# A hybrid decoder layer on one core: block order at the mixer's input, held layer-norm steps and held attention heads

## Chip, core and metric

The kernel runs on one core of a Trainium2 chip, in one launch. The metric is the device time of that core in microseconds (us): the median of three runs of the kernel. A profile of one further execution gives the spans of its instructions.

## The reference

One layer with x of 256 tokens by 2048 channels, float32:

```
x <- LN1(alpha*x + 0.5*SwiGLU_1(x))
x <- LN2(alpha*x + W_out [DiffAttn(x) || RWKV7(x)])
x <- LN3(alpha*x + 0.5*SwiGLU_2(x))
```

SwiGLU has 5632 hidden channels: `(silu(x @ w_gate) * (x @ w_up)) @ w_down`. One projection `w_in` makes the columns of both mixers. The differential attention has 8 heads, each with two softmaxes over causal scores with a linear bias; their difference multiplies v, and each head is normalised. RWKV7 has 16 heads of 64 channels with this state recursion over the tokens:

```
sa = einsum('bhvk,bhk->bhv', state, -kk_t)
state = state * w_t + sa[..., None] * (kk_t * a_t) + v_t[..., None] * k_t
y_t = einsum('bhvk,bhk->bhv', state, r_t)
```

The decay w, the rate a and the gate g come from a small block of low-rank columns of `w_in` (64 + 64 + 160 = 288 columns).

## The kernel before

Every float32 product is made of three matmuls of halves: the operand is cast to a high half (wh for weights, xh for activations) and the rest is kept as a low half (wl, xl); L153, L154 and L155 multiply high by high, high by low and low by high.

The weights are streamed through `Stream.block`: for each pair of 128-row tiles of a column block (512 or 288 columns wide), SP loads them (L133, three buffers `raw`), ScalarE (ACT) casts wh (L143), VectorE (DVE) subtracts wl (L146, called the split below), and TensorE (PE) runs six matmuls for the first 128 tokens (tt = 0) and, `lag` pairs later, six for the other 128 (tt = 1). wh and wl have five slots in the mixer and seven in the feed-forward parts; `buffers(nw, lag)` sets both numbers.

Beside the stream run generators: the heads of the attention (`attn_heads`, two generators of two heads for each group of four heads; g is the group) and the RWKV groups (`rwkv_group`, two groups of eight heads). `run_bg` advances them after each pair of the stream, by credits in the first part of the mixer, and in the output projection's first two parts ("even", set at L1160) by one step per pair; a count in `stream.hold` makes a generator sit out so many pairs there. `yield None` gives the turn back without a step. In the even part, PE's order is the order in which the code was written; all other engines' orders, and PE's elsewhere, are set by the scheduler. Each engine works through its own list in order, and a DMA stands in the list of the engine that issues it.

The mixer streams, in this order: the 288 low-rank columns, then the RWKV columns k (i = 1), r (0) and v (2) of group 0, then attention q/k and the rest. The rwkv groups invert triangular blocks on DVE (L834, L836, for j = 31 down to 1; U and Y are 64 x 1024 tiles), copy the transpose (L839) and send both through DRAM: ACT issues dY (L840) and dYT (L841), and, when these have landed, the gathers TT (L849) and YT (L853). L862 is the matmul that reads YT, L873 the one that reads TT.

The output projection runs in three parts over the sources (0 and 2: first attention group and first RWKV group; 1: the second attention group; 3: the second RWKV group). L1136 adds the residual to the first part's accumulator. In the last part `ln_stats` (L330 add, L332 statistics) and `ln_tail` (L337 to L361) normalise: two rounds of centring (L345) and scaling (L353), and each scaled quarter y is transposed by PE (L83), cast (L89, xh) and its rest subtracted (L90, xl).

Of the kernel before, what the change touches and what calls it, by code (L numbers as in the profile page):

```python
# [13 lines left out]
ALU = mybir.AluOpType  # L14
# [16 lines left out]
LAG = {"ffn": 4, "mix": 2}  # L31
NW = {"ffn": 7, "mix": 5}
# [7 lines left out]
def build(tc, A, out):  # L40
# [15 lines left out]
    def nm(s):  # L56
        uid[0] += 1
        return f"{s}_{uid[0]}"

    V, SC, G, T = nc.vector, nc.scalar, nc.gpsimd, nc.tensor  # L60
# [14 lines left out]
    def fill(n=1):  # L75
        for f in late[:n]:
            f()
        del late[:n]

    def transpose_split(src, tt, q, store, on_dve=False, put_off=False):  # L80
        tr = tr_bank[-1](True)
        for j in range(4):
            T.transpose(tr[:, j, :], src[:, j * P:(j + 1) * P], ident)  # L83
        split(tr, store, tt, q, on_dve, put_off)
# [14 lines left out]
    class Stream:  # L99
# [13 lines left out]

        def phase(self, name, pool, banks=None):
            assert not self.pend
            self.name, self.pool, self.banks, self.slot, self.rot = name, pool, banks, 0, 0
            self.buffers(NW[name], LAG[name])

        def buffers(self, nw, lag):
# [206 lines left out]
    stream = Stream()  # L326
    KX = [(k, k) for k in range(16)]

    def ln_stats(tt, y, acc, st, n):
        V.tensor_tensor(out=y, in0=y, in1=acc, op=ALU.add)  # L330
        fill(tt)
        V.bn_stats(out=st[:, n, :], in_=y)  # L332
        fill(tt)

    def ln_tail(tt, y, st, gt, bt, last):
        mv = sp.tile([P, 2], F32, tag="mv", name=nm("mv"))
        V.bn_aggr(out=mv, in_=st)  # L337
        ve = sp.tile([P, 1], F32, tag="ve", name=nm("ve"))
        V.tensor_scalar(out=ve, in0=mv[:, 1:2], scalar1=LN_EPS, scalar2=None, op0=ALU.add)
        rs = sp.tile([P, 1], F32, tag="rs", name=nm("rs"))  # L340
        G.tensor_tensor(out=rs, in0=ve, in1=neghalf, op=ALU.pow)
        fill(tt)

        def center(q):
            V.scalar_tensor_tensor(out=y[q], in0=y[q], scalar=mv[:, 0:1], in1=gt[q], op0=ALU.subtract, op1=ALU.mult)  # L345
            fill(tt)

        center(0)
        center(1)
        for q in range(4):  # L350
            c = slice(q * NB, (q + 1) * NB)
            yq = y[q]
            i = V.scalar_tensor_tensor(out=yq, in0=yq, scalar=rs, in1=bt[q], op0=ALU.mult, op1=ALU.add)  # L353
            if q < 2:
                with tc.issue_after(i.ins):
                    center(q + 2)
            if last:
                nc.sync.dma_start(out=out[tt * P:(tt + 1) * P, c], in_=yq)
            else:
                transpose_split(yq, tt, q, xT, put_off=tt == 0)  # L360
                nc.scalar.dma_start(out=xs[tt][:, c], in_=yq)  # L361
        if tt == 0 and not last:
            stream.behind = [None] * 2 + [i.ins] * 5
# [195 lines left out]
    def mix(mp, pq, C):  # L559
        vB, om = C["vB"], C["om"]  # L560

        def bank(tag, shape=(P, NB)):
            return pq.tile(list(shape), F32, tag=BANKS[tag][0], name=nm(tag), bufs=BANKS[tag][1])

        w_in = A["w_in"][0]
        R0 = 3 * AW
# [10 lines left out]
        def chan_major(acc, tt, widths, dst):  # L577
            tot = sum(widths)
            tm = mp.tile([P, NB], F32, tag="tm", name=nm("tm"), bufs=2)
            SC.copy(out=tm[:, :tot], in_=acc[:, :tot])  # L580
            tr = bank("tr", (P, 4, P))
            o = 0
            for i, w in enumerate(widths):
                T.transpose(tr[:w, i, :], tm[:, o:o + w], ident)  # L584
                o += w
            dst(tr)

        def shift(praw, i, mi, dst, n=P):
            df = mp.tile([P, S], F32, tag="itmp", name=nm("df"))
            SC.activation(out=df[:n], in_=praw[:n, i, 0:S], func=AF.Copy, scale=vB[:n, mi:mi + 1])  # L590
            x1 = praw[:n, i, 1:S + 1]
            d = df[:n]
            if len(dst.shape) == 3:
                x1 = x1.rearrange("p (c t) -> p c t", c=4)
                d = d.rearrange("p (c t) -> p c t", c=4)
            V.scalar_tensor_tensor(out=dst, in0=x1, scalar=om[:n, mi:mi + 1], in1=d, op0=ALU.mult, op1=ALU.add)
# [27 lines left out]
                SC.activation(out=g2[0:32], in_=g2[0:32], func=AF.Sigmoid)  # L624
                lora.update(tw=tw, g1=g1, g2=g2)

        stream.block(w_in, R0 + 3072, 288, KX, x_lhs, lora_done)

        res = {}

# [16 lines left out]
        def rwkv_start(g, prev=None):  # L647
            gr = Group(g)
            st = {"prev": prev, "group": gr}
            if prev is not None:  # L650
                prev["next"] = st
            st["gen"] = rwkv_group(g, st)
            stream.spawn(st["gen"], BG)
            return st

        def rwkv_cols(g, st, parts):
            gr = st["group"]

            def done(tt, acc, i):
                if tt == 0:  # L660
                    pr = hp.tile([P, 4, S + 1], F32, tag="J1" if g == 0 and i == 2 else "H3", name=nm("praw"))
                    V.memset(pr[:, :, 0:1], 0.0)
                    st["raw"] = pr
                pr = st["raw"]
                chan_major(acc, tt, [P] * 4, lambda tr: SC.copy(out=pr[:, :, 1 + tt * P:1 + (tt + 1) * P], in_=tr))
                if tt == 1:
                    for p in range(4):
                        d = (gr.rh[:, p], gr.ka[:, p], gr.vv[:, p, :])[i]
                        shift(pr, p, 8 * i + 4 * g + p, d)
                    st["rkv"[i]] = True  # L670
                    if i == 2:
                        st["gen2"] = rwkv_values(g, st)
                        stream.spawn(st["gen2"], BG)

            for i in parts:
                stream.block(w_in, R0 + i * AW + g * NB, NB, KX, x_lhs, lambda tt, acc, i=i: done(tt, acc, i))
# [320 lines left out]
        def attn_cols(g):  # L997
            st = {"q": qq[:, g],
                  "k": hp.tile([P, 4, S], F32, tag=HT["k"], name=nm("k"))}

            def qkdone(tt, acc, n):
                chan_major(acc, tt, [P] * 4, lambda tr: SC.copy(out=st[n][:, :, tt * P:(tt + 1) * P], in_=tr))
                if n == "q" and tt == 1:
                    st["left"] = 2
                    st["gens"] = [attn_heads(g, st, (i, i + 2)) for i in range(2)]
                    for x in st["gens"]:
                        stream.spawn(x, AT)

            stream.block(w_in, AW + g * NB, NB, KX, x_lhs, lambda tt, acc: qkdone(tt, acc, "k"))
            stream.block(w_in, g * NB, NB, KX, x_lhs, lambda tt, acc: qkdone(tt, acc, "q"))  # L1010
            return st

        def attn_heads(g, st, heads):
            q, k = st["q"], st["k"]
            W = 3 * P
            spans = [slice(0, P), slice(P, W)]
            for h in heads:
# [23 lines left out]
                for qb in range(2):  # L1041
                    V.tensor_scalar(out=s[:, 0, spans[qb]], in0=s[:, 0, spans[qb]], scalar1=rr[:, qb, 0:1], scalar2=None, op0=ALU.mult)
                    V.scalar_tensor_tensor(out=s[:, 0, spans[qb]], in0=s[:, 1, spans[qb]], scalar=rr[:, qb, 1:2],
                                           in1=s[:, 0, spans[qb]], op0=ALU.mult, op1=ALU.add)
                yield 0.6
                tr = bank("at", (P, 4, P))
                for b in range(3):
                    T.transpose(tr[:, b, :], s[:, 0, b * P:(b + 1) * P], ident)
# [35 lines left out]
                for qb in range(2):  # L1084
                    T.transpose(tr[:, qb, :], ot[:, qb, :], ident)
                V.tensor_scalar(out=q[:, h, :], in0=tr[:, 0:2, :].rearrange("p a b -> p (a b)"), scalar1=C["ng"], scalar2=None, op0=ALU.mult)
                yield 0.6
            st["left"] -= 1
            if st["left"] == 0:
                res[g] = q  # L1090
# [2 lines left out]
            return [g for st in sts for g in [st.get("gen"), st.get("gen2")] + st.get("gens", []) if g is not None]  # L1093

        r1 = rwkv_start(0)
        rwkv_cols(0, r1, (1, 0, 2))
        r2 = rwkv_start(1, r1)
        a1 = attn_cols(0)
        rwkv_cols(1, r2, (1, 0))
# [3 lines left out]
        a2 = attn_cols(1)  # L1103
# [16 lines left out]
        st = [sp.tile([P, 4, 6], F32, tag=f"st{t}", name=nm("st"), bufs=1) for t in range(2)]  # L1120
# [10 lines left out]
        def o_done(tt, acc, n, i):  # L1131
            c = slice(n * NB, (n + 1) * NB)
            if i == 0:
                rc = mp.tile([P, NB], F32, tag="tm", name=nm("rc"), bufs=2)
                nc.scalar.dma_start(out=rc, in_=xs[tt][:, c])
                V.scalar_tensor_tensor(out=y[tt][n], in0=rc, scalar=ALPHA, in1=acc, op0=ALU.mult, op1=ALU.add)  # L1136
            elif i < len(parts) - 1:
                V.tensor_tensor(out=y[tt][n], in0=y[tt][n], in1=acc, op=ALU.add)
            else:
                ln_stats(tt, y[tt][n], acc, st[tt], n)  # L1140
                if n == 3:
                    ln_tail(tt, y[tt], st[tt], gb[0], gb[1], False)

        y = []
# [8 lines left out]
            for n in range(4):  # L1153
                stream.block(A["w_out"][0], n * NB, NB, ks, o_lhs, lambda tt, acc, n=n, i=i: o_done(tt, acc, n, i))

        stream.hold = {g: 2 * i + 2 for i, g in enumerate(a2["gens"])}
        for i, qs in enumerate(parts):
            for q in qs:
                ready(q)
# [85 lines left out]
```

## Time and profile before

| | us |
|---|---|
| runs | 1914.72, 1918.86, 1919.4; median 1918.86 |
| profiled execution | 1916.35, span of its instructions 1914.6 |
| TensorE (PE) idle in the span | 30.6 |
| mean clock granted to TensorE | 0.994 of full speed |

A row of a timeline has the start (us from the span's start), the length, the engine, the line, the operation, the tiles as out<-in, shapes, and in brackets the idle time ahead of it with what ended it. ACTq is ACT issuing a DMA. A row of windows has the stretch, its length, then for PE, PE's weight loads, DVE, ACT and POOL the busy time and the number of instructions, the granted PE clock, the share of the DMA engines and the GB/s. PE's matmuls are pipelined, so their rows overlap.

### The profile page before, as it was taken

How to read it: one execution, taken by the hardware profiler on the slowest of the kernel's cores; microseconds unless marked ns; L12 is line 12 of the kernel's file. 1: busy time of each engine (PE TensorE's matmuls, PEld its weight loads, DVE VectorE, ACT ScalarE, POOL GpSimd, SP SyncE). 2: the span in 40 equal slices, each digit the busy share in tenths (PEclk: the TensorE clock that was granted, in tenths of full speed). 3: DMA queues.
4: the chain of work that ended last, by engine and by line, in shares of the span. 5: the costliest groups of instructions: out<-in, count | busy, mean ns of one | idle time of the engine just before them, and what ended most of it. 6: DMA issues, size and time to landing. Idle time of an engine off the chain costs nothing.

```text
span 1914.6 us, 24935 instructions
## 1 busy us (share of the span) xinstructions
PE 1884.0 (98%) x9335; PEld 1549.9 (81%) x9335; DVE 1624.3 (85%) x1834; ACT 1094.7 (57%) x1376; POOL 72.7 (4%) x110
## 2 busy tenths in 40 slices
PE   9999999999999999999999999999999999999997
PEld 7888888888888888887778778788888888888886
DVE  8999987789999976777678777999999778999995
ACT  6656664556666536656554544566666545666651
POOL 0000101100000000000000000000000110000000
PEclk9999999999999999999999999999999999999999
DMA  9756676665667456555435545775566676566743
GB/s 313 247 200 217 187 239 220 229 215 200 217 212 232 144 171 199 167 161 150 143 117 159 162 145 193 262 247 198 200 210 226 218 235 211 196 210 209 232 151 132
DMA packets 207320, 381.72 MB, mean 199 GB/s; under 512 B 23530, under 2 KB 25648, under 8 KB 206944
## 3 DMA queue, kind: packets, MB, share of 16 engines
q1 hardware_dynamic: 182928, 350.53, 55.4%
q0 software_dynamic: 6832, 15.32, 3.0%
q10 hardware_dynamic: 17440, 14.29, 2.6%
q8 instruction: 73, 1.20, 0.2%
q14 instruction: 47, 0.39, 0.1%
HBM read 368.29 MB, written 11.80 MB: 199 GB/s over the span
## 4 chain that ended last, share of the span: by engine, by line
PE 58%; DVE 3%; DMA 1%; issue 1%; ACT 1%; ACTq 0%; DVEq 0%
PE acc L154 17%; PE acc L153 17%; PE acc L155 17%; DVE wl L146 1%; PE sm L789 1%; DVE y L345 0%; PE tr L443 0%; DVE y L353 0%; PE tr L584 0%; PE at L1027 0%; PE pr L731 0%; DMA U<-dU 0%; PE sm L898 0%; PE sm L890 0%; DMA dY<-Y 0%
## 5 line engine op out<-in xcount | busy, mean ns | idle before, releaser
L143 ACT CAST wh<-raw 128x1024 fp32r<-128x1024 f32 (+2 forms) x833 | 853.6, 1049 | 597.4 <-PE acc L155 379.2
L146 DVE TENSOR_TENSOR wl<-raw,wh 128x1024 fp32r<-128x1024 f32 (+2 forms) x833 | 984.6, 1216 | 206.7 <-ACT wh L143 202.5
L154 PE MATMUL acc<-wl,xh 128*128 128x512 f32 (+1 forms) x1552 | 606.2, 392 | 2.0 <-DVE wl L146 2.0
L155 PE MATMUL acc<-wh,xl 128*128 128x512 f32 (+1 forms) x1552 | 604.3, 391 | 0.4 <-DVE xl L90 0.4
L153 PE MATMUL acc<-wh,xh 128*128 128x512 f32 (+1 forms) x1552 | 600.0, 394 | 2.0 <-ACT xh L89 1.8
L153 PEld LDWEIGHTS acc<-wh,xh 128*128 128x128 f32 x1552 | 292.6, 189 | 63.4 <-ACT xh L89 2.8
L154 PEld LDWEIGHTS acc<-wl,xh 128*128 128x128 f32 x1552 | 292.8, 189 | 61.8 <-DVE wl L146 3.6
L155 PEld LDWEIGHTS acc<-wh,xl 128*128 128x128 f32 x1552 | 292.7, 189 | 60.6 <-issue 0.7
L224 DVE TENSOR_TENSOR raw<-raw,raw 128x2048 f32<-128x2048 f32 x112 | 256.3, 2288 | 2.2 <-DMA raw<-in_ffn_w_gate_dram 1.7
L154 PE MATMUL acc<-wl,hh 128*128 128x512 f32 x544 | 212.0, 390 | 0.0
L155 PE MATMUL acc<-wh,hh 128*128 128x512 f32 x544 | 211.4, 389 | 0.0
L153 PE MATMUL acc<-wh,hh 128*128 128x512 f32 x544 | 210.9, 390 | 0.0
L153 PE MATMUL acc<-wh,s 128*128 128x512 f32 x448 | 174.9, 390 | 1.0 <-ACT acc L250 1.0
L155 PE MATMUL acc<-wh,s 128*128 128x512 f32 x448 | 174.6, 390 | 0.0
L154 PE MATMUL acc<-wl,s 128*128 128x512 f32 x448 | 174.5, 389 | 0.0
L153 PEld LDWEIGHTS acc<-wh,hh 128*128 128x128 f32 x544 | 102.1, 188 | 21.7 <-ACT wh L143 0.4
L154 PEld LDWEIGHTS acc<-wl,hh 128*128 128x128 f32 x544 | 102.2, 188 | 21.1
L155 PEld LDWEIGHTS acc<-wh,hh 128*128 128x128 f32 x544 | 102.2, 188 | 20.9
L153 PEld LDWEIGHTS acc<-wh,s 128*128 128x128 f32 x448 | 84.1, 188 | 19.1 <-ACT acc L250 1.5
L154 PEld LDWEIGHTS acc<-wl,s 128*128 128x128 f32 x448 | 84.1, 188 | 17.6 <-DVE wl L146 0.3
L155 PEld LDWEIGHTS acc<-wh,s 128*128 128x128 f32 x448 | 84.1, 188 | 17.4
L237 ACT COPY acc<-acc 128x512 f32<-128x512 f32 x28 | 16.0, 571 | 50.8 <-PE acc L155 47.0
(264 smaller groups left out, 1098.3 us busy)
## 6 DMA issues: line engine op xcount, KB each, us to landing
raw<-in_ffn_w_up_dram SPq DMA_DIRECT2D x176, 512.0 KB, 5.3
raw<-in_ffn_w_down_dram SPq DMA_DIRECT2D x176, 512.0 KB, 5.3
raw<-in_ffn_w_gate_dram SPq DMA_DIRECT2D x175, 512.0 KB, 4.6
raw<-in_w_in_dram SPq DMA_DIRECT2D x96, 512.0 KB, 3.6
raw<-in_w_out_dram SPq DMA_DIRECT2D x32, 512.0 KB, 4.1
sd<-s POOLq DMA_DIRECT2D x16, 256.0 KB, 4.0
s<-sd POOLq DMA_DIRECT2D x16, 256.0 KB, 5.1
xs<-y ACTq DMA_DIRECT2D x16, 256.0 KB, 2.5
```

The source lines that it names most:

```text
L143: SC.copy(out=wh[:, c, :w], in_=raw[:, c, :w])
L146: self.cut = V.tensor_tensor(out=wl[:, c, :w], in0=raw[:, c, :w], in1=wh[:, c, :w].bitcast(F32), op=ALU.subtract).ins
L153: T.matmul(a, hi, wh[:, j, :w], start=first and j == 0, stop=False, skip_group_check=True)
L154: T.matmul(a, hi, wl[:, j, :w], start=False, stop=False, skip_group_check=True)
L155: i = T.matmul(a, lo, wh[:, j, :w], start=False, stop=last and j == 1, skip_group_check=True)
L224: V.tensor_tensor(out=out, in0=x, in1=y, op=ALU.subtract)
L237: SC.copy(out=u, in_=a)
L789: T.matmul(pe[e][:, c, :], BK[r, p, c, e:e + 2].rearrange("p a t -> p (a t)"), AR[r, p, c].rearrange("p a t -> p (a t)"), start=True, stop ...
```

## The change

Six edits. (1) At the start of a phase the slot number of wh and wl goes on from where it was, modulo five, instead of 0. (2) In LN2, the second token half's last add and its last two statistics operations are held until the first half's second scaling has been issued (`stream.scaled`). (3) At the mixer's input the key block of 512 columns comes first, with a lag of four pairs; the block of 288 columns is second, then r and v. (4) The heads of the second attention group stop ahead of their transposes until the even part has begun. (5) At the end of a head of that group (of its first two heads) stand three yields for one. (6) The counts in `stream.hold` are one lower.

```diff
         def phase(self, name, pool, banks=None):
-            self.name, self.pool, self.banks, self.slot, self.rot = name, pool, banks, 0, 0
+            self.name, self.pool, self.banks, self.slot, self.rot = name, pool, banks, self.slot % NW["mix"], 0
...
-    def ln_stats(tt, y, acc, st, n):
-        V.tensor_tensor(out=y, in0=y, in1=acc, op=ALU.add)
-        fill(tt)
-        V.bn_stats(out=st[:, n, :], in_=y)
-        fill(tt)
+    def ln_stats(tt, y, acc, st, n, behind=None):
+        def held(on):
+            return tc.issue_after(behind) if on and behind is not None else ExitStack()
+
+        with held(n == 3):
+            V.tensor_tensor(out=y, in0=y, in1=acc, op=ALU.add)
+            fill(tt)
+        with held(n >= 2):
+            V.bn_stats(out=st[:, n, :], in_=y)
+            fill(tt)
...
+            if q == 1 and tt == 0:
+                stream.scaled = i.ins
...
-        stream.block(w_in, R0 + 3072, 288, KX, x_lhs, lora_done)
...
                 yield 0.6
+                while g == 1 and not stream.even:
+                    yield None
                 tr = bank("at", (P, 4, P))
                 for b in range(3):
                     T.transpose(tr[:, b, :], s[:, 0, b * P:(b + 1) * P], ident)
...
-                yield 0.6
+                for i in range(3 if g == 1 and h < 2 else 1):
+                    yield 0.6
...
         r1 = rwkv_start(0)
-        rwkv_cols(0, r1, (1, 0, 2))
+        stream.buffers(NW["mix"], NW["mix"] - 1)
+        rwkv_cols(0, r1, (1,))
+        stream.buffers(NW["mix"], LAG["mix"])
+        stream.block(w_in, R0 + 3072, 288, KX, x_lhs, lora_done)
+        rwkv_cols(0, r1, (0, 2))
...
-                ln_stats(tt, y[tt][n], acc, st[tt], n)
+                ln_stats(tt, y[tt][n], acc, st[tt], n, stream.scaled if tt == 1 and n >= 2 else None)
...
-        stream.hold = {g: 2 * i + 2 for i, g in enumerate(a2["gens"])}
+        stream.hold = {g: 2 * i + 1 for i, g in enumerate(a2["gens"])}
```

Lines of the changed kernel that are spoken of: L840, L842 and L845 are the inversion and the copy (L834, L836, L839 before), L846, L847, L855 and L859 the DMAs dY, dYT, TT and YT, L868 the matmul on YT (L862 before), L879 the one on TT, L1149 the residual's add (L1136 before), L334 and L337 the norm's add and statistics, L350 and L358 centring and scaling, L1048, L1049 and L1056 a head's scaling, its difference of softmaxes and its transposes.

The places where the lists of the built programs differ most follow. A row has the line, the operation, tiles as out<-in with the numbers of the buffers, and the size.

**The end of the second group's inversion, on DVE.** Before (y_9223 stands later in the list):

```order
L836 TENSOR_TENSOR Y_8112<-Y_8112,itmp_8454 64x2x30
L146 TENSOR_TENSOR wl_9228<-raw_9225,wh_9227 128x1024
L1033 TENSOR_SCALAR mx_9019<-mx_9019 128x4
L834 TENSOR_TENSOR itmp_8505<-U_8110,Y_8112 64x31
L836 TENSOR_TENSOR Y_8112<-Y_8112,itmp_8505 64x31
L839 COPY U_8110<-Y_8112 64x1024
L146 TENSOR_TENSOR wl_9251<-raw_9248,wh_9250 128x1024
L1029 SCALAR_TENSOR_TENSOR s_9030<-dist,at_9034 128x384
```

The same place in the changed kernel:

```order
L1149 SCALAR_TENSOR_TENSOR y_9211<-rc_9347,acc_9219 128x512
L842 TENSOR_TENSOR Y_8112<-Y_8112,itmp_8454 64x2x30
L1080 TENSOR_SCALAR vr_9327<-ss_9326 128x2
L840 TENSOR_TENSOR itmp_8505<-U_8110,Y_8112 64x31
L1083 TENSOR_SCALAR fl_9328<-vr_9327 128x2
L1085 SCALAR_TENSOR_TENSOR fl_9328<-vr_9327,fl_9328 128x2
L842 TENSOR_TENSOR Y_8112<-Y_8112,itmp_8505 64x31
L845 COPY U_8110<-Y_8112 64x1024
L1086 TENSOR_TENSOR ars_9329<-ars_9329,fl_9328 128x4
L1087 TENSOR_TENSOR ars_9329<-ars_9329 128x2
L146 TENSOR_TENSOR wl_9526<-raw_9523,wh_9525 128x1024
```

The last two steps and the copy stood ahead of the output projection's first results; now they stand behind the add that takes the first of them (acc_9219), and the second group's first softmaxes (s_9018 and s_9030, before behind the copy in part) are ahead of them.

**The DMAs behind it, on ACT.** Before:

```order
L840 DMA dY_8104<-Y_8112 64x1024
L841 DMA dYT_8105<-U_8110 32x1024
L991 COPY v_8972<-acc_8979 128x512
L849 DMA TT_9238<-dY_8104 32x16x32
L89 CAST xh_9217<-og_8637 128x512
L849 DMA TT_9238<-dY_8104 32x16x32 x3
L853 DMA YT_9244<-dYT_8105 32x16x32 x2
L1037 ACTIVATE s_9030,ssum_9032<-s_9030,mx_9031 128x128 x2
```

In the changed kernel:

```order
L1148 DMA rc_9569<-xs_83 128x512
L143 CAST wh_9525<-raw_9523 128x1024
L846 DMA dY_8104<-Y_8112 64x1024
L847 DMA dYT_8105<-U_8110 32x1024
L855 DMA TT_9226<-dY_8104 32x16x32 x4
L859 DMA YT_9232<-dYT_8105 32x16x32 x2
L874 COPY Q<-AR_6648 64x16x64 x2
L1058 COPY pT_9405<-at_9401 128x384
```

The softmax of s_9030 stood behind YT and now stands ahead of dY; between the four DMAs nothing else is left. On PE, the matmul that reads YT (L862 before, L868 now) stands in both programs behind the same 12 weight matmuls: six for acc_9231 (now acc_9219), whose last one ends that accumulation, and six for the next accumulator.

**LN2, on DVE.** The names y_9223 and y_9224 (before), y_9211 and y_9212 (now) are the halves' quarters of the output. Before:

```order
L332 BN_STATS st_9204<-y_9224 128x6
L332 BN_STATS st_9203<-y_9224 128x6
L337 BN_AGGR mv_10412<-st_9203 128x2
L339 TENSOR_SCALAR ve_10414<-mv_10412 128x1
L345 SCALAR_TENSOR_TENSOR y_9223<-y_9223,mv_10412,lng_10249 128x512 x2
L330 TENSOR_TENSOR y_9224<-y_9224,acc_10472 128x512
L353 SCALAR_TENSOR_TENSOR y_9223<-y_9223,rs_10416,lnb_10250 128x512
L345 SCALAR_TENSOR_TENSOR y_9224<-y_9224,mv_10412,lng_10249 128x512
L146 TENSOR_TENSOR wl_10557<-raw_10554,wh_10556 128x1024
L353 SCALAR_TENSOR_TENSOR y_9223<-y_9223,rs_10416,lnb_10250 128x512
```

In the changed kernel:

```order
L337 BN_STATS st_9191<-y_9212 128x6
L342 BN_AGGR mv_10412<-st_9191 128x2
L344 TENSOR_SCALAR ve_10414<-mv_10412 128x1
L350 SCALAR_TENSOR_TENSOR y_9211<-y_9211,mv_10412,lng_10249 128x512 x2
L358 SCALAR_TENSOR_TENSOR y_9211<-y_9211,rs_10416,lnb_10250 128x512
L350 SCALAR_TENSOR_TENSOR y_9212<-y_9212,mv_10412,lng_10249 128x512
L358 SCALAR_TENSOR_TENSOR y_9211<-y_9211,rs_10416,lnb_10250 128x512
L350 SCALAR_TENSOR_TENSOR y_9212<-y_9212,mv_10412,lng_10249 128x512
L337 BN_STATS st_9192<-y_9212 128x6
L334 TENSOR_TENSOR y_9212<-y_9212,acc_10472 128x512
```

One statistics operation, the add of acc_10472 and the split wl_10557 have left the stretch between the first half's statistics and its second scaling; the first two now follow it, and the split stands ahead of the stretch.

## The prediction

> **What bounds the kernel now.** First the page's busy shares, then TensorE's waits, then windows of 3.4 us.
>
> ```profile
> PE 1884.0 (98%) x9335; PEld 1549.9 (81%) x9335; DVE 1624.3 (85%) x1834; ACT 1094.7 (57%) x1376; POOL 72.7 (4%) x110
> ```
>
> TensorE is busy for 1884.0 of 1914.6 us. No edit changes how many matmuls there are, so only the 30.6 us of idle time, and time at a reduced clock, can move. A full weight matmul of 512 columns takes 0.229 us of the engine, read from the starts of the first and the eighth of a row of them (1.60 us / 7); the 0.39 us in a row is its length in the pipeline.
>
> ```profile
> 1087.70 0.39 PE L154 MATMUL acc<-wl,xh 128*128 128x512 f32 x1
> ...
> 1089.30 0.39 PE L155 MATMUL acc<-wh,xl 128*128 128x512 f32 x1
> ```
>
> Where the idle time lies (total us, times, longest):
>
> ```profile
> PE tr L83 <- DMA xc<-in_x_dram: 4.3, 1, 4.3
> PE at L83 <- DVE y L353: 3.3, 3, 2.3
> PE at L1027 <- DVE ot L1081: 2.4, 1, 2.4
> PE acc L154 <- DVE wl L146: 2.0, 3, 1.1
> ...
> PE at L1048 <- DVE s L1043: 1.8, 1, 1.8
> PE tr L83 <- DVE y L353: 1.5, 1, 1.5
> ```
>
> The first is the start of the program, which the change leaves alone. The L353 waits are the layer norms LN1 (about 709) and LN2 (about 1202), L1048 and part of L154 one stall near 1078, L1027 one at 1099.7. A stall costs more than its idle time, as these windows show (first columns: length, PE busy; PEclk follows POOL):
>
> ```profile
> 705.19:708.61 3.42, 3.30 (x25) 3.30 (x26) 3.39 (x9) 1.27 (x3) 0.00 (x0) 1.00 0.84 279
> 708.61:712.03 3.42, 1.31 (x9) 0.87 (x8) 3.42 (x7) 0.56 (x1) 0.99 (x1) 1.00 0.46 143
> 712.03:715.44 3.41, 3.34 (x15) 3.33 (x16) 3.26 (x6) 1.20 (x3) 0.00 (x0) 0.50 0.47 173
> 1077.26:1080.67 3.41, 1.18 (x11) 0.79 (x8) 2.53 (x7) 3.41 (x8) 0.00 (x0) 1.00 0.00 0
> 1080.67:1084.08 3.41, 3.24 (x8) 2.56 (x9) 2.39 (x3) 2.18 (x6) 0.00 (x0) 0.50 0.58 172
> 1097.73:1101.14 3.41, 1.99 (x23) 1.29 (x21) 3.07 (x11) 1.63 (x5) 1.01 (x1) 1.00 0.54 163
> 1101.14:1104.55 3.41, 2.42 (x13) 1.82 (x14) 2.51 (x9) 0.00 (x0) 0.00 (x0) 1.00 0.62 196
> 1200.13:1203.54 3.41, 0.65 (x4) 0.42 (x4) 3.41 (x6) 2.35 (x3) 0.73 (x1) 1.00 0.09 33
> 1203.54:1206.95 3.41, 2.47 (x7) 1.46 (x8) 3.41 (x6) 0.73 (x2) 0.00 (x0) 0.50 0.56 145
> 1206.95:1210.37 3.42, 3.42 (x11) 2.85 (x12) 3.42 (x6) 1.53 (x2) 0.00 (x0) 0.50 0.70 247
> ```
>
> On this grid of 3.41 us, a window with PE busy 1.31, 1.18 or 0.65 is followed by one at half clock, the one with 1.99 by one at full clock. A half-clock window that is busy loses 1.7 us. So the losses before are: LN1 2.1 idle + 1.7 + about 0.9 ahead of it (the 703 to 706 row below) = 4.7; the stall at 1078 2.2 + 0.2 + 1.7 = 4.1; L1027 2.4; LN2 2.8 + 0.9 + two half-clock windows 3.4 = 7.1.
>
> **The change part by part.** Lines of the changed kernel unless said otherwise.
>
> *A, LN1 into the mixer.* DVE decides here; three of its rows, and one window:
>
> ```profile
> 703.90 0.76 DVE L146 TENSOR_TENSOR wl<-raw,wh 128x576 fp32r<-128x576 f32 x1
> ...
> 709.91 0.75 DVE L353 SCALAR_TENSOR_TENSOR y<-y,rs,lngb 128x512 f32<-128x512 f32 x1
> ...
> 1202.93 1.22 DVE L146 TENSOR_TENSOR wl<-raw,wh 128x1024 fp32r<-128x1024 f32 x1
> ```
>
> ```profile
> 703.00:706.00 3.00, 2.16 (x16) 1.69 (x15) 2.98 (x6) 2.81 (x6) 0.00 (x0) 1.00 0.89 243
> ```
>
> Before, five pairs of the 288-column block cover the second token half's norm: 30 matmuls at 0.13 us (25 PE instructions in the 705.19 window, 0.137 each) are 4 us. With the key block first, 30 at 0.229 are 6.9 us, 2.9 more. But each of the five splits takes 1.14 us from start to start (1202.93 to 1204.07, in the rows of LN2 below) instead of 0.67 (703.90 to 704.57, where the next row begins), and they stand ahead of the scaling at 709.91: it comes 2.4 us later, at 712.3. The first xl comes one longer split or so later too, so the idle time at the block's start grows from 0.84 to some 1.4; the idle time ahead of the second half shrinks from 2.1 to some 1.6, and with over half of its window busy the clock should hold (-1.7). 3.0 is lost instead of 4.7: **-1.7**, between -4 (all hidden) and 0 (half-clock window stays).
>
> *B, order of the RWKV groups' first part.* The block order moves DVE's and ACT's background steps by a few places. A split behind such a run has cost at most 1.1 (the L154 row above), and group 0's transposed inverse may come late by part of a DMA leg. Not to be read from before: 0 to 5, I take **+1.5**, near the 1.1.
>
> *C, the stretch in which group 1's inversion runs.* Rows of 20 us:
>
> ```profile
> 1025.00:1045.00 20.00, 19.69 (x97) 15.94 (x96) 19.14 (x42) 10.18 (x16) 0.00 (x0) 1.00 0.43 131
> 1045.00:1065.00 20.00, 20.00 (x95) 15.93 (x94) 19.39 (x41) 9.65 (x12) 0.95 (x1) 1.00 0.68 207
> ```
>
> DVE has 1.5 us free in 40. In the new order the inversion begins some three pairs later and ends five or six later, and the softmax tails of two heads (L1039 to L1043 before: 1078.10 to 1079.57 in the rows below, 1.5 us each) now stand inside it: 3 us into 1.5 of room. Splits come 1 to 4 us late: **+2** (0 to 4).
>
> *D, the end of the inversion.* This decides. ACT before, then DVE before, and the flights of the DMAs that touch dY and YT:
>
> ```profile
> 1066.74 0.48 ACTq L840 DMA_DIRECT2D dY<-Y  x1
> ...
> 1071.26 0.32 ACTq L849 DMA_DIRECT2D TT<-dY  x1
> ...
> 1073.34 2.82 ACTq L853 DMA_DIRECT2D YT<-dYT  x2
> 1076.21 0.40 ACT L1037 ACTIVATE s<-s,mx 128x128 f32<-128x128 f32 x1 [3.96 <-DMA YT<-dYT]
> ```
>
> ```profile
> 1066.53 0.18 DVE L836 TENSOR_TENSOR Y<-Y,itmp 64x31 f32<-64x31 f32 x1
> 1066.74 1.14 DVE L839 COPY U<-Y 64x1024 f32<-64x1024 f32 x1
> ...
> 1078.10 0.18 DVE L1039 RECIPROCAL rr<-ssum 128x4 f32<-128x4 f32 x1 [5.04 <-ACT s L1037]
> ...
> 1079.57 3.49 DVE L146 TENSOR_TENSOR wl<-raw,wh 128x1024 fp32r<-128x1024 f32 x3
> ```
>
> ```profile
> DMA to landing us min/median/max: 3.6/4.3/7.1
> ```
>
> ```profile
> DMA to landing us min/median/max: 1.9/2.8/3.7
> ```
>
> Before, the 4.1 us at 1078 come from ACT's queue: a softmax (L1037) stands behind the YT issue. After, that softmax has left this place: -4.1. But the order shows a new wait. DVE's last inversion steps and U copy (L842, L845) stand behind L1149 y_9211<-acc_9219, ACT issues dY and all that follows behind it, and TensorE has only six weight matmuls between acc_9219's last one and L868, which reads YT. Before, 13.5 us lay between YT's landing (1076.21) and its reader. With t0 the end of acc_9219:
>
> - L1149 0.61 (1088.36 to 1088.97 below), two L842 0.21 each (1066.53 to 1066.74, L836 before) and one L840 about the same, three operations on 128x2 at about 0.08, and the wake-up: dY is issued at t0 + 1.7. ACT's cast of wh_9525 waits for the slot that the six matmuls free (t0 + 1.4), and the DMA behind it went 0.2 after such a cast began, so it adds nothing.
> - dY's issue to TT's issue 4.52 (1066.74 to 1071.26), the four TT issues 2.08 (to 1073.34), YT's issue to ACT's release 2.87: t0 + 11.2.
> - TensorE stands at L868 from t0 + 6 x 0.229 = 1.4: idle **9.8**. At least two full windows are idle, so it restarts at half clock; the rest of one window and now and then the next: 1.5 by the 1.7 a window above.
>
> ```profile
> 1088.36 0.69 DVE L1136 SCALAR_TENSOR_TENSOR y<-rc,acc 128x512 f32<-128x512 f32 x1 [0.85 <-PE acc L155]
> 1088.97 0.42 DVE L1068 TENSOR_SCALAR ot<-at 128x256 f32<-128x256 f32 x1
> ```
>
> Sum: 9.8 + 1.5 - 4.1 = **+7.2**. With the shortest landings of the two rows (3.6 and 1.9) the chain is 1.9 shorter, with the longest (7.1 and 3.7) 3.5 longer: +5.3 to +10.7, and +12.5 with two half-clock windows.
>
> The Trainium skill bears on this chain ("DMA: Bandwidth & Descriptors", Anatomy of one DMA): a transfer costs about 2.0 us whatever its size, plus its bytes at 436 GB/s. An estimate from that page is 2.6 us for the 256 KB of dY where the trace has 4.5, and 2.2 for 64 KB of YT where it has 2.9, so D would be 2.6 smaller; the page's fit is for the GpSimd path, and the trace's rows decide.
>
> *E, later start of the last heads.* The wait L1027<-L1081 arises because a head's scores follow the head before too closely. The held count and the two added yields put the scores steps later: **-2.4** (to 0, if the new distance is again too small).
>
> *F, LN2.* DVE before:
>
> ```profile
> 1201.01 0.68 DVE L330 TENSOR_TENSOR y<-y,acc 128x512 f32<-128x512 f32 x1
> 1201.61 0.74 DVE L353 SCALAR_TENSOR_TENSOR y<-y,rs,lnb 128x512 f32<-128x512 f32 x1
> ...
> 1204.07 0.75 DVE L353 SCALAR_TENSOR_TENSOR y<-y,rs,lnb 128x512 f32<-128x512 f32 x1
> ```
>
> The second token half's add (0.60, the first row to the next) and one statistics operation (about the same) leave the path ahead of 1201.61: 1.2 earlier. A split (1.14) that stood between the two scalings is now done ahead of the norm, so the second comes 2.4 earlier. Against it, 24 instead of 30 matmuls (1.4 us) cover the second half's norm, whose own chain comes 2.3 earlier. Idle time 3.7 falls by 1.2 to 2.4, one of two half-clock windows may go, some cover is lost: **-2** (-4.5 to +1). The carried slot number takes no instruction away: 0.
>
> Sum: -1.7 + 1.5 + 2 + 7.2 - 2.4 - 2 = **+4.6**. On the profiled execution, 1916.35 (span 1914.6), that is 1921. The three runs have 1914.72, 1918.86 and 1919.4; two lie 2.5 to 3 above the profiled one, so I put the sum on the median: 1923.
>
> **The rivals.**
>
> 1. *Slower, clearly.* DVE falls behind in C by 4 and t0's chain meets long landings (dY 7.1, YT 3.7) and two half-clock windows: D +12.5, C +4, others as above: +12, about 1931. For it: DVE had 5% room there, and the weight loads share the DMA engines (share 0.68 in the 1045 row). Against: with TensorE standing still, loads soon stop for want of buffers.
> 2. *Faster: the pause pays for itself.* While TensorE waits, DVE, ACT and the loads run ahead with the weights; A, E and F are then hidden fully. From the point where LN2 loses under 1 us (F -6.5), with A -3, D +5.3, E -2.4, B and C 0: -6.6, about 1912. For it: LN2's chain is DVE's, 100% busy there. Against: only five slots hold splits, so DVE can run 5 pairs ahead and no more, and 120 us lie between the places.
> 3. *Short legs.* Both legs land like the shortest ones of the two flight rows (3.6, 1.9), since the loads have stopped; D is +5.3 and, if C costs nothing either, the sum is +0.7: about 1920. For it: 0.09 of the DMA share in the 1200 row, where TensorE waits too. Against: the 4.5 of dY was measured with loads running, and in the new order its first microseconds still share the engines with them. The page of the Trainium skill named under D speaks for it.
> 4. That the change does less than it says can be left out for D: the order of the built program shows it.
>
> **How the numbers follow.** About 0.3% (5.8 us) is what can be told from no change. The forecast (+4.6, own range 0 to +9) gets 0.50: 0.30 of it within 0.3%, 0.20 slower. Rival 1: 0.23, slower. Rival 2: 0.15, faster. Rival 3: 0.12 (0.08 within, 0.02 on each side). Sums: faster 0.17, same 0.38, slower 0.45. The range 1911 to 1936 leaves out the ends of rivals 1 and 2.
>
> **What would show it.** Right: a wait of some 10 us of TensorE at L868 on YT (or on the DMA), half clock behind it, no wait at L1056 on L1049 and none at L1033; about 3 us lost at LN1 with the clock at 1.00. Wrong: the wait at L868 under 5 us, or its place taken by DVE's splits spread over 1030 to 1080; LN2 losing over 8 or under 1 us.

## The result, and the profile after

| | before | changed | ratio of the runs (95% interval) |
|---|---|---|---|
| median of 6 runs, us | 1918.88 | 1930.12 | 1.0063 (1.0052 to 1.0074) |
| profiled execution, us (span) | 1916.35 (1914.6) | 1930.98 (1929.2) | |

The changed kernel is 0.63% slower, about 11 us. Its page, first line, and its TensorE waits (total us, times, longest):

```profile
PE 1888.6 (98%) x9335; PEld 1550.7 (80%) x9335; DVE 1624.2 (84%) x1834; ACT 1093.2 (57%) x1376; POOL 74.8 (4%) x110
```

```profile
PE sm L868 <- DMA YT<-dYT: 12.1, 3, 9.7
...
PE at L83 <- DVE y L358: 4.3, 4, 2.1
PE acc L153 <- ACT xh L89: 3.3, 4, 1.2
PE acc L153 <- DVE y L334: 1.2, 1, 1.2
...
PE tr L83 <- DVE y L358: 0.8, 1, 0.8
PE acc L154 <- DVE wl L146: 0.5, 1, 0.5
```

The waits at L1027 and L1048 of before have no successor here, and a new one of 12.1 us stands on top. TensorE's idle time is 1929.2 - 1888.6 = 40.6 us, 10.0 more than before; the rest of the increase of the span by 14.6 is in the half clock. The second group's inversion ended at 1090.4 (start of the copy of U) instead of 1066.7. The residual's add and the step of the inversion behind it on DVE, then the chain on ACT and on TensorE:

```profile
1089.05 0.67 DVE L1149 SCALAR_TENSOR_TENSOR y<-rc,acc 128x512 f32<-128x512 f32 x1
1089.65 0.20 DVE L842 TENSOR_TENSOR Y<-Y,itmp 64x60 f32<-64x60 f32 x1
```

```profile
1090.27 1.05 ACT L143 CAST wh<-raw 128x1024 fp32r<-128x1024 f32 x1 [0.67 <-PE acc L155]
1090.35 0.48 ACTq L846 DMA_DIRECT2D dY<-Y  x1
1091.44 0.34 ACTq L847 DMA_DIRECT2D dYT<-U  x1
1094.55 2.08 ACTq L855 DMA_DIRECT2D TT<-dY  x4
1096.72 1.86 ACTq L859 DMA_DIRECT2D YT<-dYT  x2
```

```profile
1099.96 2.34 PE L868 MATMUL sm<-YT,Q 32*32 32x32 f32 x64 [9.72 <-DMA YT<-dYT]
```

The clock goes with it (windows; the number after POOL is the granted clock):

```profile
1092.26:1095.67 3.41, 0.00 (x0) 0.00 (x0) 1.25 (x3) 0.00 (x0) 0.00 (x0) 0.50 0.71 217
...
1099.08:1102.50 3.42, 2.40 (x66) 2.23 (x67) 0.17 (x1) 0.26 (x1) 0.00 (x0) 0.50 0.15 24
1102.50:1105.91 3.41, 3.41 (x10) 2.73 (x10) 1.21 (x2) 2.31 (x3) 0.00 (x0) 0.50 0.02 5
```

dY's issue to TT's issue is 4.20, TT's four issues 2.17, YT's issue to the matmul 3.24. TensorE stands still for 9.72 us and then works for 5.95 us at half clock (1099.96 to 1105.91).

The first group has the same wait in small, at 893.9, and a half-clock window behind it:

```profile
893.85 0.24 PE L868 MATMUL sm<-YT,Q 32*32 32x32 f32 x2 [0.78 <-DMA YT<-dYT]
896.09 1.19 PE L868 MATMUL sm<-YT,Q 32*32 32x32 f32 x62 [1.58 <-DMA YT<-dYT]
```

```profile
894.29:897.70 3.41, 1.83 (x68) 1.57 (x67) 0.37 (x1) 1.32 (x2) 0.00 (x0) 1.00 0.94 133
897.70:901.11 3.41, 3.41 (x10) 2.65 (x9) 2.23 (x3) 3.24 (x5) 0.00 (x0) 0.50 0.02 4
```

LN1 into the mixer, rows of TensorE that waited (the window of 715.09 to 718.50 ran at 1.00, as did the next):

```profile
707.63 0.47 PE L153 MATMUL acc<-wh,xh 128*128 128x512 f32 x1 [1.17 <-DVE y L334]
715.56 0.63 PE L83 MATMUL tr<-ident,y 128*128 128x128 f32 x4 [0.79 <-DVE y L358]
716.86 0.50 PE L153 MATMUL acc<-wh,xh 128*128 128x512 f32 x1 [0.68 <-ACT xh L89]
```

and LN2, first and second token half:

```profile
1214.88 0.90 PE L83 MATMUL at<-ident,y 128*128 128x128 f32 x4 [2.10 <-DVE y L358]
1216.46 0.79 PE L153 MATMUL acc<-wh,xh 128*128 128x512 f32 x1 [0.68 <-ACT xh L89]
...
1227.07 0.63 PE L83 MATMUL at<-ident,y 128*128 128x128 f32 x4 [0.68 <-DVE y L358]
1228.38 0.50 PE L153 MATMUL acc<-wh,xh 128*128 128x512 f32 x1 [0.68 <-ACT xh L89]
...
1230.86 0.63 PE L83 MATMUL at<-ident,y 128*128 128x128 f32 x4 [1.31 <-DVE y L358]
```

The second half cost little before (0.38 and 0.23 us of idle time at 1216.82 and 1218.15); now it costs 2.7.

To place all of it, the table gives what TensorE lost in each stretch: from the start of each matmul to the start of the next, less the median of that distance for matmuls of its line and shape in the same run, summed. It counts idle time and half clock together. The stretches are in us of each kernel's own span, so the later ones lie a few us apart; columns are before, changed, and the experiments that are told below.

| stretch | before | changed | e1 | e2 | e3 | e6 | e9 | e10 |
|---|---|---|---|---|---|---|---|---|
| 0 to 80 (start) | 3.2 | 5.2 | 3.8 | 3.6 | 3.6 | 3.4 | 3.5 | 3.3 |
| 690 to 730 (LN1) | 5.6 | 4.4 | 6.1 | 6.3 | 5.7 | 4.2 | 5.5 | 5.6 |
| 730 to 890 | 3.2 | 2.1 | 4.6 | 2.0 | 2.0 | 2.1 | 3.1 | 3.3 |
| 890 to 1010 | 6.3 | 10.2 | 6.0 | 10.9 | 9.8 | 11.3 | 7.4 | 6.3 |
| 1010 to 1072 | 1.3 | 2.3 | 0.8 | 2.3 | 2.4 | 2.4 | 0.6 | 0.7 |
| 1072 to 1120 | 7.7 | 13.6 | 3.7 | 18.2 | 12.5 | 4.4 | 7.6 | 7.7 |
| 1120 to 1190 | 2.3 | 3.3 | 3.9 | 3.5 | 5.4 | 10.7 | 3.3 | 2.3 |
| 1190 to 1245 (LN2) | 8.4 | 10.4 | 10.7 | 8.3 | 9.6 | 10.5 | 8.5 | 8.6 |

The 5.2 at the start of the changed kernel's profiled execution is hardly the change's, which leaves that part alone: the twelve experiments have 3.1 to 5.0 there, with no order by kernel. The profiled execution of before, 1916.35, also lies below the median of its runs. So the spans differ by 14.6 us and the medians by 11.2.

### The profile page after: what moved, and what is told of

Its sections match the earlier page's. It is cut to its first block, busy times and chain, and to the rows that moved or that the text cites. A ratio compares the mean times of both kernels' runs of the same rounds, so it can differ in the third digit from the quotient of the medians.

```text
span 1929.2 us, 24939 instructions
## 1 busy us (share of the span) xinstructions
PE 1888.6 (98%) x9335; PEld 1550.7 (80%) x9335; DVE 1624.2 (84%) x1834; ACT 1093.2 (57%) x1376; POOL 74.8 (4%) x110
```

## The experiments

The kernel before and the changed kernel differ in six edits, and the first runs take them apart. "Changed" is the changed kernel. All ratios are against runs of the kernel before on the same chip.

**e1, the old block order, all other edits kept.**

```diff
-        stream.buffers(NW["mix"], NW["mix"] - 1)
-        rwkv_cols(0, r1, (1,))
-        stream.buffers(NW["mix"], LAG["mix"])
-        stream.block(w_in, R0 + 3072, 288, KX, x_lhs, lora_done)
-        rwkv_cols(0, r1, (0, 2))
+        rwkv_cols(0, r1, (1, 0, 2))
```

(with the 288-column block back at its old place)

> The changed kernel with the old block order (288 columns first), all other edits kept. Theory 1 (the block order delays the second group's inversion past the residual's add, and that makes the wait at the matmul on YT): no wait of TensorE on YT, neither the 9.7 us in the second group nor the 2.4 us in the first; time 10 to 14 us below the changed kernel, near 1918, which is within 4 us of the kernel before. Theory 2 (the held heads and their extra yields crowd DVE and delay the inversion): the wait on YT stays, over 6 us, and the time stays over 1925.

Measured: 1918.49, ratio 0.9999 (0.9991 to 1.0008). There is no wait on YT among the waits, neither in the first nor in the second group, and the copy of U starts at 1068.8. Theory 2 falls; edit 3 makes the wait. (Edit 3 is the block order together with the lag of four pairs in the key block; no run parts the two.) The stretch 1072 to 1120 loses 3.7, less than before: the stall at L1027 is gone. Of the one near 1078, 1.6 us of idle time are left of 2.4, as waits for a cast wh and a split.

**e2, the new block order alone** (the reverse: the kernel before with edit 3 only).

> The kernel before with the new block order alone (key block first, lag 4). Theory 1: TensorE waits 8 to 11 us for YT in the second group and 1 to 4 us in the first; 8 to 13 us slower than before. The stall at L1027 on L1081 of 2.4 us may go with it or stay. Theory 2: no wait on YT above 2 us, and the time within 3 us of before.

Measured: 1932.48, ratio 1.0073 (1.0061 to 1.0086). Its waits:

```profile
PE sm L861 <- DMA YT<-dYT: 12.9, 3, 10.1
...
PE at L1026 <- DVE ot L1080: 2.5, 1, 2.5
```

(L861 is the matmul on YT and L1026 the heads' scores in this kernel.) Edit 3 alone gives the whole loss; the old stall at the heads' scores is still there beside the new one, and the ratio lies within the changed kernel's interval. The stall near 1078 is gone without the heads' edits.

**e3, without the held norm steps** (edit 2 taken out of the changed kernel).

> The changed kernel without the held add and statistics of LN2. Theory A (the held steps shorten cover of the second token half and cost more there than they gain): the idle time of TensorE ahead of the second half's first weight matmuls falls from some 2.7 us to under 1, and the time is 1 to 3 us below the changed kernel. Theory B (LN2 lost more because of what came before it, the held steps gain 1 to 2 us as I forecast): 1 to 3 us above the changed kernel.

Measured: 1930.10, ratio 1.0057 (1.0045 to 1.0069), the same as the changed kernel within the intervals. The second token half's idle time fell from 2.7 to 0.6, as theory A has it, but the first half's wait for its first scaling (L353 in this kernel) grew from 2.1 to 3.7:

```profile
PE at L83 <- DVE y L353: 4.3, 2, 3.7
```

**e10, the held norm steps alone** (edit 2 added to the kernel before).

> The kernel before with the held norm steps of LN2 alone. Theory A (they cost cover of the second half): LN2 loses 10 to 11 us instead of 8.4 and the time is 1.5 to 3 us above before. Theory B (my forecast): LN2 loses 5 to 7 us, 1 to 4 us below before. Theory C (a wash, as the two pairs of runs on the new order say): within 1 us.

Measured: 1918.58, ratio 1.0000 (0.9990 to 1.0011); LN2 loses 8.6 against 8.4. Theory C: the edit changes nothing in the time. My forecast of a gain falls, and so does theory A as a price. In this kernel the loss doesn't move to the second token half (0.61 and 0.23 us of idle time there, 0.38 and 0.23 before). TensorE's wait for the first scaling falls from 2.3 to 1.3, about what I had forecast, but the split stays between the scalings, now ahead of the second one, and TensorE waits for it:

```profile
PE acc L154 <- DVE wl L146: 3.5, 3, 1.7
...
PE at L83 <- DVE y L358: 1.5, 2, 1.3
```

The longest wait of each row is LN2's.

**e4, TT's gathers on GpSimd's queue.**

```diff
-                nc.scalar.dma_start(out=TT[rr, :, cc], in_=dY[uu].rearrange("u s t -> s u t"))
+                nc.gpsimd.dma_start(out=TT[rr, :, cc], in_=dY[uu].rearrange("u s t -> s u t"))
```

> The changed kernel with the four gathers TT issued by GpSimd instead of ACT, so that YT's issue no longer stands behind them and behind the landing of dY; in the new order the copy of U also comes ahead of the residual's add on DVE. Theory 1 (the wait at the matmul on YT is this chain, link by link): the chain loses the 2.1 us of the TT issues and some 1 to 1.5 us more, the wait falls from 9.7 to 5.5 to 7 us, and the time by 2.5 to 4.5 us below the changed kernel. Theory 3 (the wait is set by the DMA queue or by YT's own transfer): the wait stays above 9 us.

Measured: 1929.21, ratio 1.0054 (1.0042 to 1.0067). YT's issue came 3.4 us after dYT's instead of 5.3:

```profile
1085.17 0.48 ACTq L846 DMA_DIRECT2D dY<-Y  x1
...
1087.62 0.34 ACTq L847 DMA_DIRECT2D dYT<-U  x1
...
1090.99 0.87 ACTq L859 DMA_DIRECT2D YT<-dYT  x2
```

```profile
1097.49 1.99 PE L868 MATMUL sm<-YT,Q 32*32 32x32 f32 x64 [8.75 <-DMA YT<-dYT]
```

```profile
DMA to landing us min/median/max: 3.7/6.2/6.4
```

The second is TensorE, the third the flights of YT's DMAs in this run. The wait fell by 1.0 instead of 3 to 4: YT was issued earlier, but took up to 6.4 us to land (2.3 to 5.7 over the four in the changed kernel) while the four TT transfers and the weight loads were on their way. Both theories were half right: the chain is what TensorE waits for, but its last link is not a fixed time. The Trainium skill ("DMA: Bandwidth & Descriptors", Issuing engines are not separate DMA queues) says that DMAs of all engines end up on the same 16 DMA engines and interleave, and that a second issuing engine saves issue time only; this run agrees as far as the issue goes, with YT issued 1.9 us sooner behind dYT. That TT's transfers made YT's flight some 3 us longer isn't shown: in the changed kernel's second group YT landed 2.3 to 3.1 us after issue with the four TT transfers still in flight.

**e7, YT ahead of TT on ACT's queue.**

```diff
             for e in range(2):
-                nc.scalar.dma_start(out=YT[64 * e:64 * e + 32], ...
+                ydma = nc.scalar.dma_start(out=YT[64 * e:64 * e + 32], ...
+            with tc.issue_after(ydma.ins):
+                for d, e, rr, cc, uu in quad:
+                    nc.scalar.dma_start(out=TT[rr, :, cc], in_=dY[uu].rearrange("u s t -> s u t"))
```

> The changed kernel with YT's two DMAs issued ahead of TT's four, on the same ACT queue. In the run with TT on GpSimd the YT transfer took 6.2 to 6.4 us instead of 2.3 to 3.5, with TT's transfers beside it. Theory 4 (the transfers of TT slow YT's, since both go through the same DMA engines in short rows): YT now starts when dYT has landed, some 2.5 us earlier than in the changed kernel, and lands in 2 to 3.5 us; the wait falls from 9.7 to 6.5 to 7.5 us and the time by 2 to 4 us. Rival (YT's landing was slow there for another reason, such as the quiet loads starting again): YT takes over 5 us here too and the wait stays above 8.5.

Measured: the wait in the second group fell from 9.72 to 7.79:

```profile
1098.62 2.29 PE L869 MATMUL sm<-YT,Q 32*32 32x32 f32 x64 [7.79 <-DMA YT<-dYT]
```

YT was issued at 1095.39, so the two DMAs took 3.2 us to the matmul, as in the changed kernel and not as in e4. That fits theory 4, although the wait ended 0.3 above the expected band, but it doesn't settle it: in the first group YT is issued ahead of TT in the changed kernel too, and its DMAs landed 3.8 and 5.7 us after issue there, 3.9 and 5.6 here. What sets YT's flight stays open. The time did not follow: 1929.72, ratio 1.0073 (1.0055 to 1.0090), while the stretch 1072 to 1120 lost 9.3 instead of 13.6. LN2 lost 1.3 more in this run; the rest of the difference stays open.

**e5, the edits on the heads alone** (4, 5 and 6 added to the kernel before).

> The kernel before with the edits on the heads alone (transposes of the second group held until the even part, three yields for one, counts one lower); block order, norm and slots as before. Theory 1 (these edits remove the stalls at 1078 and at L1027 and cost nothing): the waits L1048<-L1043 and L1027<-L1081 are gone, the stretch from 1072 to 1120 loses 3.5 to 4 us instead of 7.7, and the time is 2 to 5 us below the kernel before. Rival (what they free is lost at the next wait, as the old-order run suggests with its 1.6 us more in 1120 to 1190 and 1.4 in 730 to 850): within 2 us of before.

Measured: 1914.85, ratio 0.9989 (0.9979 to 1.0000). The waits at L1027 and L1048 are gone and 1072 to 1120 loses 4.8. But at the place of the stall near 1078 TensorE now waits for a cast and then 0.80 us for a split, no less than the 2.4 us of idle time before:

```profile
PE acc L153 <- ACT wh L143: 2.2, 2, 2.0
```

And 1120 to 1190 loses 5.5 against 2.3. Most of what was saved in the one reappears in the other, as the rival said; the 0.11% that the time shows lies at the edge of the interval.

**e11, the heads' edits with the carried slot number** (edit 1), to see what separated e1 from e5.

> The edits on the heads and the carried slot number, with the old block order and without the held norm steps. The run with all edits but the block order was 1918.5, the one with the heads' edits alone 1914.9. If the held norm steps make that difference: 1914 to 1916 here. If the carried slot does: 1917.5 to 1919.5.

Measured: 1917.33, ratio 0.9995 (0.9986 to 1.0004), between the two bands. With e10 that says that neither edit 1 nor edit 2 alone has a price that these runs can tell from zero.

The traces do show where edit 1 acts. In LN2 the split that stands between the two scalings in the kernel before and in e5 is done ahead of the norm here, and TensorE's wait for the first scaling is 3.7 instead of the 2.3 of e5:

```profile
PE at L83 <- DVE y L353: 4.3, 2, 3.7
```

The same wait over the kernels (but e6, whose norm meets other waits): 2.3 with neither edit 1 nor edit 2 (before, e2, e5, e9, e12), 3.4 to 3.7 with edit 1 alone of the two (e3, e8, e11), 1.3 with edit 2 alone (e10), 2.1 with both (the changed kernel, e1, e4, e7).

**e6, the matmul on YT written four pairs later.**

```diff
-            yield 0.6
+            for i in range(5 if g == 1 else 1):
+                yield 0.6
             if g == 1:
                 yield from transposed()
```

> The changed kernel with five yields for one ahead of the second group's steps behind the YT issue, so that some 15 us of TensorE's work, instead of 1.4, stand between the end of the first output accumulation and the matmul on YT. Theory 1: the wait of 9.7 us falls below 2 us and the half-clock windows there go; time 8 to 11 us below the changed kernel, 1919 to 1922. Rival (the lost time is DVE's, which is overloaded in this stretch, and shows at another wait): the wait on YT goes, but other waits take over 5 us of it, and the time stays above 1925.

Measured: 1929.45, ratio 1.0060 (1.0043 to 1.0078). The wait in the second group is gone, and 1072 to 1120 loses 4.4 instead of 13.6. But 1120 to 1190 loses 10.7 instead of 3.3:

```profile
PE acc L153 <- ACT xh L89: 5.2, 4, 2.7
...
PE sm L869 <- DMA YT<-dYT: 3.3, 2, 2.6
```

```profile
1143.37 0.50 PE L153 MATMUL acc<-wh,xh 128*128 128x512 f32 x1 [1.23 <-ACT xh L89]
1186.37 0.69 PE L153 MATMUL acc<-wh,xh 128*128 128x512 f32 x1 [2.67 <-ACT xh L89]
```

The row of YT is now the first group's alone. The row at 1186.37 is the first matmul of the output projection's last part, which needs the second RWKV group's result. The rival's numbers came true: of 9.2 us taken off, 7.4 came back. Some 5.2 of them lie at the start of the last part, 1170 to 1192, where the changed kernel loses 0.1. The other 2.3 belong to the row at 1143.37, which the changed kernel has as well (1.23 us, at 1156.63): there the clock stayed at full speed behind it, here a half-clock window followed. Whether the rival's reason holds is open: no wait is one for a split, but DVE, which makes the tile og from which that xh is cast, was busy for 3.31 of the 3.41 us ahead of 1186.37. Read from the code, and not measured, the second group's last step is written behind pair 134 of the stream in the changed kernel and the last part begins behind pair 136, so four pairs of cover put in front of the chain are taken away from behind it. That fits a chain from the inversion to the last part's input that is too late as a whole, and then moving one reader only moves a part of the wait.

**e8, the same without the held norm steps.**

> The run with the later matmul on YT, and without the held norm steps. If those cost 2 us in LN2, as 10.4 and 10.7 us lost there with them against 8.4 without them say (but one run without them lost 9.6): 1 to 2 us below the run with the later matmul. If they cost nothing: within 1 us of it.

Measured: 1930.02, ratio 1.0068 (1.0052 to 1.0084): as e6, and once more no price of edit 2.

**e9, late first steps under the old block order.** In the new order the first RWKV group cannot start before the low-rank columns, which are now second. This kernel has the old order, and makes the group wait as long:

```diff
-            while "tw" not in lora:
+            while "tw" not in lora or (g == 0 and "k" not in st):
                 yield None
```

> The kernel before, whose first RWKV group now also waits for the key block before its first step. In the code each step of both groups is then written behind the same pair of the stream as in the changed kernel (first step behind pair 26 instead of 18, the second group's DMAs behind pair 78, its copy of U behind pair 88), with the old block order. Theory 5 (the late first step, behind the block of low-rank columns, makes the second group's chain late): a wait on YT of over 4 us and 5 to 12 us slower than before. Theory 6 (it is the place that the scheduler gives the chain in the engines' lists under the new block order; the built lists here have the second group's last mask matmul two rows ahead of its place before, and 54 rows ahead of that in the changed kernel): no wait on YT over 1 us, the inversion's end within 5 us of 1066, time within 4 us of before.

Measured: 1916.46, ratio 0.9986 (0.9975 to 0.9997). No wait on YT; the copies of U (durations in ns, then the first and the last start in us):

```profile
L839 DVE COPY U<-Y x2: 1040/1090/1141, 868.5 to 1065.1; 64x1024 f32<-64x1024 f32 x2
```

Theory 5 falls. By the code, every step of both groups is written behind the same pair as in the changed kernel, and yet the second group's inversion ends at 1065.1 and not at 1090.4. What differs is the place in the engines' lists: by the traces the last mask matmul ahead of the inversion is the 5004th of TensorE's 9335 matmuls here and before (start at 1011.6 and 1012.8), and the 5057th in the changed kernel (1028.8). That is the scheduler's doing under edit 3. By which of its rules it comes about isn't shown by these runs.

**e12, e9 with the heads' edits.**

> The heads' edits and the late first steps of the first RWKV group together, old block order. Theory 6: no wait on YT, time 1913 to 1917. Theory 5: a wait on YT of over 4 us, over 1920.

Measured: 1916.04, ratio 0.9983 (0.9974 to 0.9991): no wait on YT. This is the lowest ratio of the study, about 3 us below before and 15 below the changed kernel; e9 and e5 lie within its interval.

## Why the prediction was right, and where its sizes were off

The forecast was 1923, slower, with a rival at 1931; measured 1930.12. The direction and the wait that decides (D) are those forecast. The sum fell short by 7 us in the medians: +11.2 lies outside the forecast's own range of 0 to +9, and +4.6 lay within the 5.8 us that the prediction couldn't tell from no change.

- **D, the wait at L868.** Idle 9.8 forecast, 9.72 measured; dY issued at t0 + 1.7 forecast, and 1.3 after the add's start (1089.05) measured; dY's leg 4.5 against 4.20, TT's issues 2.1 against 2.17, YT's 2.9 against 3.24. That the idle time came out to within 0.1 us is in part luck, since these differences cancel. The first row of flights from which the range was taken was misread: 3.6/4.3/7.1 mixes dY's two DMAs (3.8 and 4.4 us by themselves) with the TT gathers, and 7.1 is a gather's, so no dY landed that late. The half clock behind it cost two windows instead of the one and a bit I took (1.5): by the last two windows above, 2.4 x 0.5 + 1.7 = 2.9. The estimate of 2.6 us for dY from the Trainium skill ("DMA: Bandwidth & Descriptors", Anatomy of one DMA), whose fit is for the GpSimd path, is not borne out on ACT's queue: dY landed 4.1 us after its issue.
- **E, L1027.** -2.4 forecast; the wait is gone in the changed kernel, in e1 and e5, and there in e2: right. That the stall near 1078 goes was put under D, and rightly: e2 is without it, while e5 keeps its idle time. D and E together: +4.8 forecast, 13.6 - 7.7 = +5.9 measured.
- **B, the first part of the groups.** This term was mis-sized: "0 to 5, I take +1.5, near the 1.1". 730 to 1010 lost 12.3 instead of 9.5, +2.8, and the +3.9 in 890 to 1010, against -1.1 in 730 to 890, is the same wait on YT in the first group, 2.4 idle and a half-clock window. I had bounded it by a DMA leg, but gave the clock no term there.
- **F, LN2.** The wrong one: "-2 (-4.5 to +1)", measured +2.0 in this pair of profiles, and LN2's loss of over 8 us was one of the signs that I had named for being wrong. The first token half's first scaling was to come 1.2 earlier; TensorE waited 2.10 for it instead of 2.33. A split that left the stretch stands on the same engine just ahead of it, with no gap between the rows, so its 1.14 us were still on the path (the fourth row is the first scaling):

```profile
1209.22 1.21 DVE L146 TENSOR_TENSOR wl<-raw,wh 128x1024 fp32r<-128x1024 f32 x1
1210.35 1.28 DVE L334 TENSOR_TENSOR y<-y,acc 128x512 f32<-128x512 f32 x2
1211.66 0.69 DVE L337 BATCH_NORM_STATS2 st<-y 128x6 f32<-128x512 f32 x1
...
1214.08 0.75 DVE L358 SCALAR_TENSOR_TENSOR y<-y,rs,lnb 128x512 f32<-128x512 f32 x1
```

The second half, whose cover fell from 30 to 24 matmuls, now waits 2.7 us. Two steps failed: "is now done ahead of the norm", which I costed as free without looking at what DVE did there, and "the carried slot number takes no instruction away: 0". By e11 against e5 it is edit 1 that moves the split, and with it alone the wait for the first scaling is 1.4 us longer; edit 2 does take 1.0 to 1.6 off that wait. In the time neither shows.
- **A, LN1.** -1.7 forecast, -1.2 in the profile. Idle 1.17, 0.79 and 0.68 were to be 1.4 and 1.6, and the clock held. But other runs with the same block order lost 4.2 to 6.3 there, and runs with the old order about 5 to 6: not a gain that shows in the time.
- **C.** +2 forecast, +1.0 measured. TensorE lost little; the inversion began 12.4 us later (1037.1 instead of 1024.8) and took 53 us instead of 42, since some 5 us more of softmax steps and two more splits (2.5 us) stood between its steps in DVE's list. The two make the 24 us by which it ended later.
- The sum: F alone is 4.0 of what was missing, B 1.3, D and E 1.1, A 0.5; C was 1.0 too high. The loss of 1120 to 1190 (+1.0) had no term; the waits of 1.2 and 0.3 us there come with the heads' edits (the changed kernel, e1, e5, e11 and e12 have them, before, e2, e9 and e10 don't).
- **The rivals.** The time came to that of rival 1, but with only one of its conditions, the two half-clock windows: C was not 4, and the landings were not long. Rival 2, that the pause pays for itself, had 0.15 and did not happen: LN2 lost more, not less. Rival 3 needed short legs; e7 shows what a shorter chain gives at L868, about 2 us of wait, and that even that is not found again in the time.
- What I did not see is e6's point: I treated L868 as a wait by itself. It is where a late chain is met first, and filling it brought more than half of the loss back at the next reader.

## What to carry to other kernels

When a change moves the order in which blocks of work are written, look in the built lists for the long dependent chain that has the fewest places to hide, and measure its start and end against its reader; here the lists, with durations from the trace of before, gave a new 10 us wait with each link of its chain within 0.4 us. In e6 a wait on a late chain wasn't cured by moving its reader: count the cover from the chain's start to its last reader as one sum. And where an engine works without a gap ahead of a latency path, an operation taken out of the path and put in front of it on the same engine still delays it, as the split in LN2 did.

## What the runs showed of the hardware that was not expected

- The flight of the same small transfer varied threefold. YT's DMAs (64 KB each, in rows of 128 bytes) landed 1.9 us after issue at the fastest (before) and 6.4 at the slowest (e4). TT's transfers beside them don't explain it alone: in the changed kernel YT took 2.3 and 3.1 us behind four TT in flight, and 3.8 and 5.7 issued ahead of them.
- Which idle window costs a half-clock window isn't set by the busy time of the rows alone. On the 3.41 us grid, the windows at full clock with TensorE busy for under 1.5 us were each followed by one at half clock in all fourteen traces. Between 1.5 and 2.05 both happened: 1.83 us was followed by 0.50 in e5 (at 1142.42) and by 1.00 in e1 (at 1201.85), neither with 32 by 32 matmuls. Above 2.05 the clock held, but for one window of 2.40 in e3 (at 893.59), most of whose matmuls were 32 by 32, as were those of the one at 894.29 above. What decides between them wasn't tried.
